# Channel mixers' up panels with tokens stationary, 512 columns each, and results turned and sent by way of the DRAM

## The chip, the cores and the metric

The kernel runs on one core of one Trainium2 chip. Its time is the device time of one execution in microseconds; a lower time is better. The core has a matrix engine (TensorE, PE in the profile, with its weight loads as PEld), a vector engine (VectorE, DVE), a scalar engine (ScalarE, ACT), GpSimd (POOL) and a queue engine that starts most transfers (SyncE, SP). They run side by side and wait for each other on semaphores; each runs its own instructions in the order in which they were built.

## The reference

A trunk of two layers for 256 tokens of width 2048, in float32. The first layer mixes tokens with gated linear attention (GLA), the second with forgetting attention (FoX); both also attend to 256 memory tokens. After each comes a channel mixer, a gated MLP with a causal convolution over three tokens:

```python
def causal_dwconv(u, w, b):
    s_ = u.shape[1]
    up = jnp.pad(u, ((0, 0), (CONV_WIDTH - 1, 0), (0, 0)))
    return w[0] * up[:, 0:s_] + w[1] * up[:, 1:s_ + 1] + w[2] * up[:, 2:s_ + 2] + b

def conv_ffn(h, w_up, conv_w, conv_b, w_down):
    u = causal_dwconv(h @ w_up, conv_w, conv_b)
    a, val = split_cols(u, [FFN_HIDDEN, FFN_HIDDEN])
    return (jax.nn.silu(a) * val) @ w_down

def reference(x, mem, ...):
    mem_n = rmsnorm(mem, norm_mem)
    for i in range(DEPTH):
        if i == N_A_LAYERS:
            fk, fv, fc = fox_shared_kv(x, fox_kv_norm, fox_w_kv, fox_b_f)
        mk, mv = memory_kv(mem_n, mem_w_kv[i])
        h = rmsnorm(x, norm_mix[i])
        ...
        h = rmsnorm(x, norm_ffn[i])
        x = x + conv_ffn(h, ffn_w_up[i], ffn_conv_w[i], ffn_conv_b[i], ffn_w_down[i])
    return rmsnorm(x, norm_final)
```

`h` is 256 x 2048, `w_up` 2048 x 11264 (5632 gate columns, then 5632 value columns), `w_down` 5632 x 2048.

## The kernel before

**Number form.** Every float32 operand of the large products is split in a high part, which TensorE multiplies directly, and the low rest. A product is high x high + high x low + low x high. Activations are kept split as sixteen chunks of 128 inputs (`bufA`, `bufB`, both parts of a chunk side by side, 2 x 256 tokens). Weights are streamed: `split_unit` (L188 to L207) loads a unit of 128 x 1024 numbers into `raw` on SP's queue (L200), copies it to the high part `whi` on ScalarE (L205) and takes the difference `wlo` on VectorE (L206). `raw`, `whi` and `wlo` have four buffers each. `tc.high_priority(offset=AHEAD)` puts the splits ahead in the order that the scheduler builds, so they run before the matmuls that need them.

**Two forms of a product.** `proj_fm` (through `panels_fm`) keeps weights stationary: for a panel of 256 output columns, a unit holds four chunks; the high weights meet both parts of a chunk in one matmul with 512 moving columns (L242), the low weights meet the high part with 256 (L240). The result has columns on partitions and tokens along the row, as high and low sums side by side, which `whole` adds up with one copy on ScalarE (L252) and one addition on VectorE (L254). `proj_tm` keeps 128 tokens stationary: a unit holds two chunks of 512 output columns, which are the moving operand, three matmuls for each chunk and token block (L286). The result has tokens on partitions. `panel_tm` (L311) is the same product in steps of one unit, so that two panels can be interleaved.

**The channel mixer** (`ffn`). The hidden width is done in three parts, `PARTS`, of 16, 16 and 12 blocks of 128. In each part the up panels run first, one for each block, with the block's 128 gate columns and 128 value columns. Their eviction `up_out` adds the halves (`whole`), multiplies with the row of norm factors `nx.row()` (L1038), convolves along the tokens with one ScalarE operation (L1042) and two on VectorE (L1043, L1044), applies SiLU (L1047), multiplies the gate with the value (L1048) and splits the product into the chunk `m[i]` (L352, L353). Then come four down panels of 512 columns, `add_out` with `proj_tm`, which add to the residual `x` (L322). The first three up panels of a mixer are interleaved by `three_fm`, so that the last four chunks of `h` are met late: those come out of the projection just before, through `preparing`.

**Turning.** `preparing` takes each column group `f` (512 columns) of the residual as it is finished, transposes 32 x 32 blocks on VectorE (L1077) and moves the blocks to their partitions with sixteen small DMAs on SP's queue (`move`, L466), then splits them into four chunks (L363, L365). `move_far` (L472, L475), used in the FoX stage, does the same by one DMA to DRAM and four back; SP waits for the first before it starts the four.

**PSUM.** Eight banks: four for `acc`, two for `ps_s`, one each for `ps_o` and `ps_t`.

**The order.** The matmuls stand in program order as far as the scheduler keeps it; `tc.issue_after(i)` puts an instruction behind another one in the built order. After the first mixer comes the FoX stage (keys, values, queries, attention, output projection), then the second mixer and the final norm.

Of the kernel before, what the change touches and what calls it, by code (L numbers as in the profile page):

```python
# [19 lines left out]
P = 128  # L20
# [34 lines left out]
def _panels():  # L55
# [6 lines left out]
    def fm(key, w, c0, kcs=full, second=None):  # L62
        cols = [(c0, 256)] if second is None else [(c0, 128), (second, 128)]
        out.append((key, w, kcs, cols, 4))
# [76 lines left out]
def _trunk(ctx: ExitStack, tc: tile.TileContext, xt, xtok, memt, wp, wgu, gns, gfin, cnv, par, msk, out):  # L141
# [40 lines left out]
    loads, casts, ends = [], [], []  # L182
# [6 lines left out]
    def split_unit(unit, pool=wpool, pieces=1, before=None):  # L189
# [3 lines left out]
        with tc.high_priority(offset=AHEAD):  # L193
# [7 lines left out]
            for i in range(pieces):  # L201
# [4 lines left out]
                V.tensor_tensor(lo[:, s], raw[:, s], hi[:, s].bitcast(F32), ALU.subtract)  # L206
# [86 lines left out]
    def panel_tm(key, src, evac):  # L293
# [24 lines left out]
        return step  # L318

# [149 lines left out]
    def move_far(pool, dst, src, n):  # L469

        far = pool.tile([P, 4 * T], F32, name="far", tag="far", bufs=2)
        nc.sync.dma_start(far[:, : 4 * n], src[:, : 4 * n])  # L472
        blocks = far[:, : 4 * n].rearrange("(q i) (c n) -> c i q n", q=4, c=4)
        for c in range(4):
            nc.sync.dma_start(dst[32 * c : 32 * (c + 1), : 4 * n].rearrange("i (q n) -> i q n", q=4), blocks[c])  # L475
# [538 lines left out]
    def add_out(key, src, then=None, spare=None, last=None, first=0):  # L1014
        for f in range(first, 4):
            def evac(b, a, f=f):
# [4 lines left out]
            proj_tm((*key, f), src, last if f == 3 and last is not None else evac, spare if f == 3 else None)  # L1021

    def ffn(l, nx, h, m, then, spare=None, last=None):
        with tc.tile_pool(name=f"ffn{l}", bufs=1) as fp:
# [6 lines left out]
            for p, (lo, hi) in enumerate(PARTS):  # L1031
                def up_out(j, i):
                    cv = {}

                    def evac(c, a):
                        u = us[turn[0] % 4]
                        turn[0] += 1
                        V.tensor_tensor(u[:, 2:], whole(a), nx.row(), ALU.mult)  # L1038
                        col = (c * 44 + j) * 4
# [6 lines left out]
                        if c == 1:  # L1046
                            S.activation(cv[0], cv[0], AF.Silu)  # L1047
                            V.tensor_tensor(r, cv[0], r, ALU.mult)  # L1048
                            split(m, i, r)
# [182 lines left out]
```

## Time and profile before

| What | Value |
|---|---|
| Median of three runs | 2262.89 us (2262.39 to 2263.41) |
| The profiled execution | 2263.27 us |
| Its span | 2261.4 us |
| TensorE clock granted, mean | 0.999 |
| Instructions | 33526 |
| HBM read | 429.31 MB, 192 GB/s over the span |

The profile was taken on one execution. The time of that execution is 1.9 us above its span, which runs from its first to its last recorded instruction. An engine's busy time counts overlapping instructions once. In lists of groups, a row gives the source line, the engine, the operation, what it writes and reads, the shape and the count, then busy time and the mean duration of one; a matmul's mean duration is longer than the distance between two, because they are pipelined. In the chain of work that ended last, a row gives the start, the length and what ran; its long TensorE pieces divided by their count give the distance of two matmuls. In windows, each engine's busy time is followed by its instruction count, then the granted clock, the share of time that the DMA engines were busy, and GB/s. In a timeline a row gives the start, the length, the engine and the instructions merged into it, and in brackets an idle time before them and what ended it. SPq is SP's queue with the issue of DMAs.

### The profile page before, as it was taken

To read this page: it belongs to the slowest core of one execution; us is meant where nothing else is said; L and a number is where in the kernel's file an instruction comes from. 1 tells how busy PE (TensorE), PEld (TensorE's weight loads), DVE (VectorE), ACT (ScalarE), POOL (GpSimd) and SP (SyncE) were. 2 spreads that over 40 slices of the span, in tenths; PEclk is the share of its full clock that TensorE was granted. 3 is DMA by queue.
4 is the path that set the end of the run, shared out by engine and by line. 5 is a ranking of instruction groups with operands and counts; after the bars stand their busy time and mean duration, and the time that the engine had idled before them with its cause. 6 is when DMAs were issued, how large, how long until landed. Compare 5 with 4: busy or idle time off the path is not lost.

```text
span 2261.4 us, 33526 instructions
## 1 busy us (share of the span) xinstructions
PE 2249.8 (99%) x12253; PEld 1967.1 (87%) x12253; DVE 1617.1 (72%) x2746; ACT 1250.7 (55%) x1986; POOL 3.4 (0%) x19
## 2 busy tenths in 40 slices
PE   9999999999999999999999999999999999999998
PEld 8889998888888888888888998888888888888887
DVE  7779877677765777557777569677776577756775
ACT  6657675555543555445555555456554455534554
POOL 0000000000000000000000000000000000000000
PEclk9999999999999999999999999999999999999999
DMA  9655554665555555555565567766656555655554
GB/s 341 198 184 166 177 168 171 214 201 190 191 196 189 190 193 188 195 188 192 189 217 202 183 192 240 229 204 218 194 189 198 188 189 191 192 194 187 191 193 147
DMA packets 142125, 444.38 MB, mean 197 GB/s; under 512 B 18428, under 2 KB 34952, under 8 KB 141832
## 3 DMA queue, kind: packets, MB, share of 16 engines
q1 hardware_dynamic: 140808, 441.05, 58.8%
q8 instruction: 96, 1.57, 0.3%
q10 hardware_dynamic: 1152, 1.19, 0.2%
q14 instruction: 69, 0.57, 0.1%
HBM read 429.31 MB, written 5.52 MB: 192 GB/s over the span
## 4 chain that ended last, share of the span: by engine, by line
PE 96%; ACT 1%; DVE 1%; DMA 1%; issue 0%; SPq 0%; DVEq 0%; ACTq 0%
PE acc L242 37%; PE acc L286 34%; PE acc L240 20%; PE acc L311 2%; PE ps_s L242 1%; PE ps_s L240 1%; DMA raw<-wp 0%; ACT whi L205 0%; DVE wlo L206 0%; PE ps_s L758 0%; PE ps_o L495 0%; PE ps_s L495 0%; PE ps_o L931 0%; PE ps_s L976 0%; ACT L822 0%
## 5 line engine op out<-in xcount | busy, mean ns | idle before, releaser
L206 DVE TENSOR_TENSOR wlo<-raw,whi 128x1024 fp32r<-128x1024 f32 (+4 forms) x809 | 968.7, 1201 | 518.5 <-ACT whi L205 429.9
L205 ACT ACTIVATE whi<-raw 128x1024 fp32r<-128x1024 f32 (+4 forms) x809 | 839.6, 1039 | 600.5 <-PE acc L286 311.2
L242 PE MATMUL acc<-B,whi 128*128 128x512 f32 x2048 | 482.6, 390 | 0.0
L242 PEld LDWEIGHTS acc<-B,whi 128*128 128x128 f32 x2048 | 378.9, 188 | 75.2
L286 PE MATMUL acc<-whi,mix 128*128 128x512 f32 x1216 | 302.5, 389 | 0.0
L242 PE MATMUL acc<-mix,whi 128*128 128x512 f32 x1224 | 298.3, 391 | 0.0
L286 PEld LDWEIGHTS acc<-whi,mix 128*128 128x128 f32 x1216 | 228.3, 188 | 47.4
L242 PEld LDWEIGHTS acc<-mix,whi 128*128 128x128 f32 x1224 | 226.0, 188 | 44.4
L240 PEld LDWEIGHTS acc<-B,wlo 128*128 128x128 f32 x2048 | 255.7, 191 | 5.3
L240 PE MATMUL acc<-B,wlo 128*128 128x256 f32 x2048 | 259.4, 283 | 0.0
L286 PE MATMUL acc<-whi,B 128*128 128x512 f32 (+3 forms) x896 | 200.5, 360 | 0.0
L286 PEld LDWEIGHTS acc<-whi,B 128*128 128x128 f32 x896 | 162.7, 188 | 15.9 <-ACT whi L205 0.3
L286 PE MATMUL acc<-wlo,mix 128*128 128x512 f32 x608 | 164.5, 389 | 0.0
L240 PEld LDWEIGHTS acc<-mix,wlo 128*128 128x128 f32 x1224 | 154.9, 191 | 6.0 <-ACT mix L363 1.6
L240 PE MATMUL acc<-mix,wlo 128*128 128x256 f32 x1224 | 157.9, 284 | 1.2 <-ACT mix L363 1.2
L286 PEld LDWEIGHTS acc<-wlo,mix 128*128 128x128 f32 x608 | 114.1, 188 | 23.7
L242 PE MATMUL acc<-A,whi 128*128 128x512 f32 x536 | 131.3, 390 | 0.0
L252 ACT ACTIVATE part<-acc 128x256 f32<-128x256 f32 x238 | 89.4, 378 | 58.8 <-PE acc L242 58.8
L242 PEld LDWEIGHTS acc<-A,whi 128*128 128x128 f32 x536 | 100.1, 188 | 20.5
L286 PE MATMUL acc<-wlo,B 128*128 128x512 f32 (+3 forms) x448 | 111.6, 360 | 0.0
L1042 ACT ACTIVATE cv<-u,cw 128x256 f32<-128x256 f32 x176 | 104.2, 595 | 4.2 <-DVE u L1038 4.1
L352 ACT ACTIVATE mix<-cv 128x256 fp32r<-128x256 f32 x60 | 25.0, 416 | 143.6 <-DVE cv L1048 143.6
(250 smaller groups left out, 1809.4 us busy)
## 6 DMA issues: line engine op xcount, KB each, us to landing
raw<-wp SPq DMA_DIRECT2D x743, 512.0 KB, 3.8
raw<-wp SPq DMA_DIRECT2D x32, 384.0 KB, 3.1
raw<-wp SPq DMA_DIRECT2D x24, 388.0 KB, 3.5
turn<-blk SPq DMA_DIRECT2D x144, 32.0 KB, 3.0
raw<-wp SPq DMA_DIRECT2D x8, 400.0 KB, 3.0
far<-y SPq DMA_DIRECT2D x6, 384.0 KB, 6.1
z<-far SPq DMA_DIRECT2D x24, 96.0 KB, 2.9
xf<-xt SPq DMA_DIRECT2D x16, 128.0 KB, 5.2
```

The lines of the kernel that those rows point to most:

```text
L205: casts.append(S.activation(hi[:, s], raw[:, s], AF.Copy))
L206: V.tensor_tensor(lo[:, s], raw[:, s], hi[:, s].bitcast(F32), ALU.subtract)
L240: mm = TE.matmul(acc[p][c][:, :T], w[:, s], both[:, 0, :], start=False, stop=end and j == 3)
L242: mm = TE.matmul(acc[p][c], w[:, s], both, start=u == j == 0, stop=end and j == 3)
L252: S.activation(t, a[:, T:], AF.Copy)
L286: mm = TE.matmul(acc[b][:, :n], src[kcs[j] - base][:, part, b * P : (b + 1) * P], w, start=u == 0 and low == part == j == 0, stop=u == end ...
L311: mm = TE.matmul(acc[b][:, :n], src[kc - base][:, part, b * P : (b + 1) * P], ready[low][:, j * n : (j + 1) * n], start=i == low == part = ...
L352: S.activation(hi, src, AF.Copy)
L1042: S.activation(r, u[:, 2:], AF.Identity, bias=w[3], scale=w[2])
```

## The change

An up panel now has 512 columns: two blocks' gate columns and the same blocks' value columns. It keeps tokens stationary, in `panel_tm`. Its result, tokens on partitions, is transposed in 32 x 32 blocks by VectorE straight from PSUM, high-priority, into one of two buffers `ys`; `far_away` writes that to DRAM with one DMA and returns a function that fetches it back with four, into one of two buffers `zs`. `close` calls that function later: behind the load of the third unit of the panel after next (`issue_after(loads[-1])`), and the convolution behind that unit's low split (`issue_after(lows[-1])`). `convolve` is the old eviction for two blocks, without `whole`; its multiplication with the norm row reads runs of 32 tokens. `ys` and `zs` take over the space of memory keys and values and of FoX's `fvt`, which are free then.

The first two up panels of a mixer are interleaved by `two_tm` in place of `three_fm`: the first six units of both, then the last two of both, with the second one's sums in `ps_s`. The first two down panels of every part are interleaved in the same way, the last unit of each held back, and the last two up panels' fetches and convolutions are put between their units (`hooks`). So the first two column groups of a part end one right after the other. Before FoX they go by `move_far` in place of sixteen small DMAs each.

```diff
         for p, (lo, hi) in enumerate(PARTS):
-            for j in range(lo, hi):
-                fm(("up", l, j), ("ffn_w_up", l), j * P, second=HID + j * P)
+            for j in range(lo, hi, 2):
+                tm(("up", l, j), ("ffn_w_up", l), j * P, 2 * P, more=[(HID + j * P, 2 * P)])
...
-                V.tensor_tensor(lo[:, s], raw[:, s], hi[:, s].bitcast(F32), ALU.subtract)
+                lows.append(V.tensor_tensor(lo[:, s], raw[:, s], hi[:, s].bitcast(F32), ALU.subtract))
...
-    def panel_tm(key, src, evac):
+    def panel_tm(key, src, evac, second=False):
...
-                acc.extend(pacc.tile([P, 512], F32, name="acc", tag="acc") for _ in range(2))
+                acc.extend(work("s", 2) if second else pacc.tile([P, 512], F32, name="acc", tag="acc")
+                           for _ in range(2))
...
+    def two_tm(steps, count, last, hooks={}):
+
+        for units in (range(count - last), range(count - last, count)):
+            for p, step in enumerate(steps):
+                for u in units:
+                    step(u)
+                    hooks.get((p, u), int)()
...
-    def move_far(pool, dst, src, n):
-
-        far = pool.tile([P, 4 * T], F32, name="far", tag="far", bufs=2)
+    def far_away(pool, src, n):
+
+        far = pool.tile([P, 4 * T], F32, name="far", tag="far", bufs=3)
         nc.sync.dma_start(far[:, : 4 * n], src[:, : 4 * n])
         blocks = far[:, : 4 * n].rearrange("(q i) (c n) -> c i q n", q=4, c=4)
-        for c in range(4):
-            nc.sync.dma_start(dst[32 * c : 32 * (c + 1), : 4 * n].rearrange("i (q n) -> i q n", q=4), blocks[c])
+
+        def back(dst):
+            for c in range(4):
+                nc.sync.dma_start(dst[32 * c : 32 * (c + 1), : 4 * n].rearrange("i (q n) -> i q n", q=4), blocks[c])
+
+        return back
+
+    def move_far(pool, dst, src, n):
+        far_away(pool, src, n)(dst)
...
+        if hooks is not None:
+            first = 2
+            two_tm([panel_tm((*key, f), src, evac_of(f), second=f == 1) for f in range(2)],
+                   len(where[(*key, 0)]), 1, hooks)
+        for f in range(first, 4):
+            proj_tm((*key, f), src, last if f == 3 and last is not None else evac_of(f), spare if f == 3 else None)
...
+            def convolve(j, i, z):
+
+                for s in range(2):
                     cv = {}
-
-                    def evac(c, a):
+                    for c in range(2):
                         u = us[turn[0] % 4]
                         turn[0] += 1
-                        V.tensor_tensor(u[:, 2:], whole(a), nx.row(), ALU.mult)
-                        col = (c * 44 + j) * 4
+                        V.tensor_tensor(by_run(u[:, 2:]), z[:, :, 2 * c + s], by_run(nx.row()), ALU.mult)
+                        col = (c * 44 + j + s) * 4
...
+            def up(j, i, second=False):
+
+                def evac(b, a):
+                    with tc.high_priority(offset=AHEAD):
+                        if b == 0:
+                            count[0] += 1
+                        y = ys[count[0] % 2]
+                        V.transpose(y[:, :, :, b, :], a.rearrange("p (k c i) -> p c k i", c=4, i=32))
+                    if b:
+                        open_.append((j, i, far_away(dp, flat(y), T)))
+
+                return panel_tm(("up", l, j), h, evac, second)
+
+            def close(left):
+
+                while len(open_) > left:
+                    j, i, back = open_.pop(0)
+                    z = zs[count[1] % 2]
+                    count[1] += 1
+                    with tc.issue_after(loads[-1].ins):
+                        back(flat(z))
+                    with tc.issue_after(lows[-1].ins):
+                        convolve(j, i, z)
+
+            for p, (lo, hi) in enumerate(PARTS):
+                js = list(range(lo, hi, 2))
                 if p == 0:
-                    first = 3
-                    three_fm([("up", l, j) for j in range(3)], h, [up_out(j, j) for j in range(3)])
-                for j in range(lo + first, hi):
-                    proj_fm(("up", l, j), h, up_out(j, j - lo))
+                    two_tm([up(j, j - lo, j > lo) for j in js[:2]], 8, 2)
+                for n, j in enumerate(js):
+                    if p == 0 and n < 2:
+                        continue
+                    step = up(j, j - lo)
+                    for u in range(8):
+                        step(u)
+                        if p == 0 and n < 4:
+                            if n == 3 and u in (0, 2):
+                                close(2 - u // 2)
+                        elif u == 2:
+                            close(1)
                 end = p == len(PARTS) - 1
-                add_out(("down", l, p), m, then if end else None, spare if end else None, last if end else None)
+                down = {"then": then, "spare": spare, "last": last} if end else {}
+                add_out(("down", l, p), m, hooks={(0, 2): lambda: close(1), (1, 4 if end else 3): lambda: close(0)}, **down)
...
-                move(z, y)
+                if far is not None and f < 2:
+                    move_far(far, flat(z), flat(y), T)
+                else:
+                    move(z, y)
```

More of the change, by code (lines that the diff above doesn't have):

```diff
@@ L1011, in fox, with add_out, evac_of @@
                     steps[f](u)
-    def add_out(key, src, then=None, spare=None, last=None, first=0):
-        for f in range(first, 4):
-            def evac(b, a, f=f):
+    def add_out(key, src, then=None, spare=None, last=None, first=0, hooks=None):
+        def evac_of(f):
+            def evac(b, a):
                 add_to(f)(b, a)
@@ L1158, in last @@
                 (nc.scalar if f == 1 else nc.sync).dma_start(out[b, :, f * 512 + lo : f * 512 + hi], t)
-        ffn(1, n, bufA, bufB, then, op, last)
+        ys, zs = ([const.tile([P, 4, 4, 2, 32], F32, name="yzu", tag=f"{t}{i}") for i in range(2)] for t in ("mk", "mv"))
+        ffn(1, n, bufA, bufB, ys, zs, then, op, last)
 def _constants():
```

46 lines of the change are left out of this document (27 added, 19 removed).

## The prediction

> **What bounds the kernel now.** I read the first part of the page, then the chain of work that ended last, then the list of who made TensorE wait.
>
> ```profile
> span 2261.4 us, 33526 instructions
> PE 2249.8 (99%) x12253; PEld 1967.1 (87%) x12253; DVE 1617.1 (72%) x2746; ACT 1250.7 (55%) x1986; POOL 3.4 (0%) x19
> PE 96%; ACT 1%; DVE 1%; DMA 1%; issue 0%; SPq 0%; DVEq 0%; ACTq 0%
> ```
>
> ```profile
> PE ps_o L180 <- DVE B L177: 1.4, 1, 1.4
> PE acc L240 <- ACT mix L363: 1.2, 1, 1.2
> PE acc L286 <- ACT whi L205: 0.7, 1, 0.7
> PE ps_s L758 <- ACT later L806: 0.3, 1, 0.3
> ```
>
> 96% of the chain is TensorE, and all its recorded waits add up to 1.4 + 1.2 + 0.7 + 0.3 = 3.6 us. So time can come only from what the stream of matmuls itself takes, and be lost only where a new wait breaks it. The next question is what one matmul costs in each form. The chain in order of time shows long pieces that nothing interrupts:
>
> ```profile
> 513.76 7.28 PE acc L242 x32
> 521.04 3.83 PE acc L240 x32
> ...
> 639.66 87.04 PE acc L286 x384
> ```
>
> The first two are one up panel of 256 columns, weights stationary: 32 matmuls with 512 moving columns at 7.28/32 = 0.2275 us, and 32 with 256 at 3.83/32 = 0.1197. The third is a down part, tokens stationary, all matmuls 512 wide: 87.04/384 = 0.2267. Twice the columns cost less than twice the time: the two up rows give (0.2275 - 0.1197)/256 = 0.42 ns a column, and so 0.1197 - 256 x 0.00042 = 0.012 us that every matmul costs whatever its width.
>
> **What is removed: matmuls.** For 512 up columns and one chunk of 128 inputs, before: four 512-wide and four 256-wide; after: six 512-wide. The streamed columns are 3072 both times; two matmuls fewer carry the fixed cost. Per layer 44 panels of 256 become 22 of 512.
> Before: 2 x 44 x (7.28 + 3.83) = 977.7 us. After: 2 x 22 x 16 x 6 = 4224 matmuls x 0.2267 = 957.4 us (by 87.04/384). **Gain 20.2 us.** It needs the down panels' rate to hold beside the up stage's busier VectorE. These two windows, down and up, speak for that:
>
> ```profile
> 640.00:724.00 84.00, 84.00 (x372) 69.60 (x371) 45.67 (x48) 35.51 (x37) 0.00 (x0) 1.00 0.57 195
> 745.00:900.00 155.00, 155.00 (x894) 137.21 (x893) 119.59 (x197) 90.19 (x140) 0.00 (x0) 1.00 0.57 190
> ```
>
> The clock is 1.00 in both, and VectorE at 77% (119.59/155) leaves the up panels at 3.83 and 7.28 us. The rate could be off by 1 ns: 4224 x 0.001 = 4 us to either side.
>
> *A rule against the change.* The Trainium skill (TensorE: Matmul & The Clock Gate, Back-to-back issue gap) puts the fixed cost of a warm matmul at 2.5 ns, not 12. By it the sum would lose almost all its gain: 2 x 16 x 22 x 2 = 1408 matmuls saved x 2.5 ns = 3.5 us. The two rows disagree with it here.
>
> **What is added on VectorE and ScalarE.** These are the groups:
>
> ```profile
> L206 DVE TENSOR_TENSOR wlo<-raw,whi 128x1024 fp32r<-128x1024 f32 x743 | 905.7, 1222 | 471.3 <-ACT whi L205 385.7 <-issue 52.0 <-PE acc L240 20.8
> L205 ACT ACTIVATE whi<-raw 128x1024 fp32r<-128x1024 f32 x743 | 784.0, 1056 | 552.9 <-PE acc L286 275.5 <-PE acc L242 143.4 <-ACT whi L205 47.0
> L254 DVE TENSOR_TENSOR wholes<-acc,part 128x256 f32<-128x256 f32 x238 | 98.9, 418 | 1.0 <-ACT part L252 0.7
> L252 ACT ACTIVATE part<-acc 128x256 f32<-128x256 f32 x238 | 89.4, 378 | 58.8 <-PE acc L242 58.8
> L1038 DVE TENSOR_TENSOR u<-wholes,row 128x256 f32<-128x256 f32 x176 | 74.0, 423 | 2.7
> L1043 DVE SCALAR_TENSOR_TENSOR cv<-u,cw,cv 128x256 f32<-128x256 f32 x176 | 83.7, 478 | 0.0
> L1077 DVE STREAM_TRANSPOSE blk<-x 128x512 f32<-128x512 f32 x24 | 16.9, 706 | 3.7 <-DMA turn<-blk 3.3
> ```
>
> Per 512 columns VectorE loses four additions in `whole` (4 x 0.418 = 1.7 us) and ScalarE four copies (4 x 0.378 = 1.5); VectorE gets two transposes, 2 x 0.706 = 1.4 us by the SBUF row. No row has a transpose that reads PSUM, or a multiplication that picks runs of 32. Bounds: as in these rows (-0.3 us on balance), or twice as long (1.4 us for the transposes, 4 x 0.423 = 1.7 for the products). At the worst VectorE has some 3 us more than before in 21.8 us of TensorE, and it idles 23% (5 us) of the up stage: hidden. I take the low end, since a transpose streams the same 512 elements from either place.
>
> **What is added on the queues.** A panel now writes 512 KB to DRAM in one DMA and fetches it back in four of 128 KB, 44 times. The FoX stage does this already:
>
> ```profile
> far<-y SPq DMA_DIRECT2D x2, 512.0 KB, 5.2
> far<-y SPq DMA_DIRECT2D x6, 384.0 KB, 6.1
> z<-far SPq DMA_DIRECT2D x8, 128.0 KB, 2.9
> raw<-wp SPq DMA_DIRECT2D x743, 512.0 KB, 3.8
> ...
> 1372.80 0.33 SPq L472 DMA_DIRECT2D far<-y  x1
> ...
> 1377.90 1.74 SPq L475 DMA_DIRECT2D z<-far  x4
> ```
>
> There SP waits in line for the write before it issues the fetches (1372.80 to 1377.90), with weight loads behind it, and none of TensorE's four waits lies there. In the up panels the waits are placed late instead. One unit of weights (two chunks) is 12 x 0.2267 = 2.72 us. Call 0 the end of a panel on TensorE. A load of unit k is free to go when the split four units earlier has given up its buffer, which waits for the matmuls eight units earlier: 1.06 + 1.22 = about 2.5 us (with the semaphores) after unit k-8 ends.
> *The write* stands after the load of the next panel's seventh unit (free at -0.2) and waits for the second transpose, about 1.5. The eighth unit's load, behind it, is free at 2.5: nothing lost. *The fetches* stand behind three more loads, the last free at 2.5 + 3 x 2.72 = 10.7; the write has landed at 1.5 + 0.4 + 5.2 = 7.1. No wait; they hold SP for 1.74 us, to 12.4, and the next load is free at 13.4. The data is back at 12.4 + 2.9 = 15.3. *The convolution* stands on VectorE behind the low half of that third unit of the second panel on, which needs the seventh unit of the next panel done (19.0), so it starts at 21.3. Behind it are the splits that TensorE needs, but it finds its data 6 us early. Steady state: **0**. If the write took more than 10.7 - 1.9 = 8.8 us, SP would hold the loads; a load has 10.9 - 2.5 - 3.8 = 4.6 us to spare before the split is late, and the split (2.3 us) has 8.2 - 2.3 = 5.9 before TensorE is. So 10.5 us of cover lie behind the 8.8.
>
> **The joints** are where it can lose.
> *Start of the second mixer.* Now:
>
> ```profile
> 1522.89 3.79 PE L242 MATMUL acc<-mix,whi 128*128 128x512 f32 x16
> 1530.94 0.50 PE L240 MATMUL acc<-mix,wlo 128*128 128x256 f32 x2 [1.19 <-ACT mix L363]
> ...
> 1525.14 11.99 SPq L466 DMA_DIRECT2D turn<-blk  x19
> 1537.23 1.96 SPq L200 DMA_DIRECT2D raw<-wp  x4
> ...
> 1541.02 1.06 ACT L205 ACTIVATE whi<-raw 128x1024 fp32r<-128x1024 f32 x1 [0.68 <-DMA raw<-wp]
> ```
>
> TensorE starts at 1522.89 and meets chunk 8 too early, at 8.1 us. After, chunk 8 is in the fifth unit, at 4 x 2.72 = 10.9: **-1.2 us**. What is late next: SP is held by 19 small moves, only seven loads stand ahead of them in the built program, and the eighth unit's high half ends at 1542.1; it is needed at 1522.89 + 7 x 2.72 + 0.24 = 1542.2. Zero to spare: 0 to 1 us, I take 0.
> *End of the last part* (both mixers). The last panel's convolution waits for unit 9 (counted from 0) of the down part's 24 (needs unit 5's buffers, 16.3 us; start 18.8). Its products and steps are 16 operations of 0.35 to 0.4 us from start to start, 6 us, among four splits of 1.2: 30.4 us. Its chunk would be due at 10 x 2.72 = 27.2, but the built order pulls up unit 12 and two thirds of 13, so the last of it is due at 33.5. Cost 0; 0 to 3 us each if the splits slip.
> *Start of FoX.* The first two down columns now end together, and go to DRAM by `move_far` one after the other. The first is ready 39 us into the part (matmuls done at 35.8; behind them on VectorE an addition, a transpose and a split): write to 45, fetches, second write 48 to 54, fetches to 56.4. Before, the third column's 16 small moves had begun by then (its matmuls end at 18 x 2.72 = 49.0, its transposes 3 us later). Now they end, with five loads between, at 68.7, 3.4 us after FoX starts (65.3), and land at 6.3; the first split of chunk 8 is done at 7.1, and it is due at 6.7. The fourth column's 16 moves follow:
>
> ```profile
> 1190.03 3.79 PE L242 MATMUL acc<-B,whi 128*128 128x512 f32 x16
> ...
> 1192.89 10.62 SPq L466 DMA_DIRECT2D turn<-blk  x16
> ...
> 1215.56 1.06 ACT L205 ACTIVATE whi<-raw 128x1024 fp32r<-128x1024 f32 x1 [2.37 <-DMA raw<-wp]
> ```
>
> They ran from 2.9 to 13.5 us after the start, and ScalarE then waited 2.37 us for a load. After, they run to about 15.5, so the loads behind come 2 us later, into a place that was already short. 0 to 5 us, I take **+2**.
>
> **Sum**, against the profiled execution's own 2263.27 us (span 2261.4 and 1.9 around it): 2263.3 - 20.2 - 1.2 + 2 = 2243.9. The median shown is 0.4 lower than that execution, so I say 2244.
>
> **Rivals.**
> *Joints dearer.* FoX's start costs 5, each last part 3, the second mixer's start 1: 12 where I took 2: about 2254. For it: margins of 0 to 3 us, several at once. Against: before, TensorE lost 1.2 us at all of these.
> *The rate does not carry over* (no change). The up panels mix evictions, transposes and 77% VectorE beside the matmuls; if a 512-wide matmul takes 977.7/4224 = 0.2315 us there, 4.8 ns above the down row, nothing is won: 2263.3 - 1.2 + 2 = 2264. For it: all of the gain is a cost of some 12 ns a matmul whose origin no row names. Against: the down window has the same form, with its splits and evictions, at 0.2267. The Trainium skill's rule above would end near this, at 2260.6.
> *SP blocks (slower).* One mechanism: the write waits for transposes and the fetches for the write on the queue that carries the weights. It decides from a write of 8.8 + 10.5 = 19 us on, or when four fetches and small moves together pass that cover; each us beyond costs 1 us per panel, and 2 us would be 88: 2263.3 - 21 + 88 = 2330; one us, 2286. Against: the longest landing here is 6.1 us for such writes (384 KB, FoX), and these add 1 MB to 21.8 us, 48 GB/s to 190, with DMA engines at 0.57.
> *It doesn't do what it says*: reload of the stationary tokens for each 512 columns is not hidden. The down part has just that, and runs at 0.2267.
>
> **How the numbers follow.** Forecast 0.73 (2244; own range 2240 to 2249), dearer joints 0.17 (2249 to 2258), no change 0.04, slower 0.06. The low end is 2263.3 - 21.4 less half of the rate's 4 us: 2240. The high end takes in the dearer joints and part of the rate: 2256. A measurement of this kernel tells 0.2%, 4.5 us, from no change. Faster 0.90, within it 0.04, slower 0.06.
>
> **What would show it.** Up pieces of the chain at 0.2267 us a matmul, 21.8 us a panel; 1408 matmuls fewer; TensorE's waits under 6 us in all, the largest at FoX's start; SP's wait for the DRAM write gone from the up panels; VectorE's multiplication not waiting for the fetch. I am wrong if the matmul with a stationary token block takes over 0.231 us there, or if TensorE waits for weight splits in each panel.

## The result and the profile after

| | Before | After |
|---|---|---|
| Median | 2263.15 us (4 runs, 2262.39 to 2264.56) | 2246.23 us (4 runs, 2244.61 to 2251.22) |
| Profiled execution | 2263.27 us | 2251.22 us |
| Its span | 2261.4 us | 2249.3 us |

The ratio is 0.9928, with a 95% interval of 0.9911 to 0.9945: 16.9 us faster. The profiled execution of after is the longest of its four, 5 us above their median; the stage where that comes from is shown below. Lines have moved by a few: after, TensorE's matmuls are L313 (tokens stationary, in steps), L285 (tokens stationary) and L241/L239 (weights stationary); the weight split is L204 (ScalarE) and L205 (VectorE); the transposes out of PSUM are L1094, the products with the norm row L1075, the write to DRAM and the fetch L482 and L487, the small moves L476, the splits of turned chunks L373 and L375.

The page of after, its span, its busy times and the chain by engine:

```profile
span 2249.3 us, 30561 instructions
PE 2232.8 (99%) x10845; PEld 1896.4 (84%) x10845; DVE 1589.9 (71%) x2658; ACT 1204.1 (54%) x1810; POOL 3.4 (0%) x19
...
PE 91%; DMA 3%; DVE 2%; ACT 2%; SPq 1%; issue 1%; DVEq 0%; ACTq 0%
```

12253 - 10845 = 1408 matmuls fewer, and TensorE is as full as before. 9% of the chain that ended last is no longer TensorE's (it was 4%); how long TensorE itself waited, the list of its waits below says. The long pieces of the chain in order of time say what an up matmul costs now:

```profile
506.05 149.60 PE acc L313 x660
...
723.65 193.12 PE acc L313 x852
```

193.12/852 = 149.60/660 = 0.2267 us: the rate of the down panels, to the last digit. The stages are told apart by the first matmul of each, in the timeline of TensorE, one row of before (its other two anchors, 1190.03 and 1522.89, stand in the prediction) and three of after:

```profile
461.39 3.79 PE L242 MATMUL acc<-B,whi 128*128 128x512 f32 x16
```

```profile
462.10 1.98 PE L313 MATMUL acc<-whi,B 128*128 128x512 f32 x8
...
1180.44 3.79 PE L241 MATMUL acc<-B,whi 128*128 128x512 f32 x16
...
1520.90 1.98 PE L313 MATMUL acc<-whi,mix 128*128 128x512 f32 x8
```

| Stage | Before, us | After, us | Difference |
|---|---|---|---|
| up to the first mixer | 461.39 | 462.10 | +0.7 |
| first mixer | 728.64 | 718.34 | -10.3 |
| FoX | 332.86 | 340.46 | +7.6 |
| second mixer to the end | 738.51 | 728.40 | -10.1 |

The 0.7 us before the first mixer lie in a part that the change leaves alone: two waits of 0.9 and 0.5 us, which the repeats below don't have, where before there was one of 0.7. The mixers gave 20.4 us and FoX, which the change does not touch but for what feeds its start, took 7.6 back. The list of who made TensorE wait, after:

```profile
PE ps_s L241 <- ACT whi L204: 1.8, 1, 1.8
PE ps_o L179 <- DVE B L176: 1.4, 1, 1.4
PE acc L239 <- ACT B L373: 1.2, 1, 1.2
PE ps_t L442 <- DVE dg L440: 1.1, 1, 1.1
PE acc L239 <- DVE wlo L205: 0.9, 1, 0.9
PE ps_s L313 <- ACT whi L204: 0.5, 1, 0.5
PE acc L285 <- ACT whi L204: 0.5, 1, 0.5
PE ps_s L778 <- ACT later L826: 0.2, 1, 0.2
```

They come to 7.6 us, where before it was 3.6. Each happens once (the second number), so none is a cost of every panel. Three of them, 1.8 + 1.2 + 1.1 = 4.1 us, are at FoX's start. The timeline of TensorE there:

```profile
1188.49 0.51 PE L239 MATMUL acc<-B,wlo 128*128 128x256 f32 x2 [1.18 <-ACT B L373]
...
1205.58 0.38 PE L442 MATMUL ps_t<-dg,onesr 128*128 128x256 f32 x1 [1.10 <-DVE dg L440]
1207.76 3.78 PE L241 MATMUL ps_s<-B,whi 128*128 128x512 f32 x8 [1.80 <-ACT whi L204]
1211.34 1.91 PE L239 MATMUL acc<-B,wlo 128*128 128x256 f32 x8
1213.05 2.42 PE L241 MATMUL acc<-B,whi 128*128 128x512 f32 x8
1215.30 1.11 PE L239 MATMUL acc<-B,wlo 128*128 128x256 f32 x8
1216.26 2.00 PE L241 MATMUL acc<-B,whi 128*128 128x512 f32 x8
```

Eight 512-wide matmuls take 3.78 us at 1207.76 and 2.00 at 1216.26; eight of 256 take 1.91 and then 1.11. Behind the waits TensorE ran slower for some 7 us: (3.78 - 2.00) + (1.91 - 1.11) + (2.42 - 2.00) = 3.0 us lost. The windows show why, in the column behind POOL's, the granted clock:

```profile
1205.00:1210.00 5.00, 2.62 (x6) 2.01 (x7) 5.00 (x8) 2.80 (x4) 0.31 (x1) 0.71 0.59 205
1210.00:1215.00 5.00, 5.00 (x19) 4.29 (x18) 1.81 (x2) 1.06 (x1) 0.00 (x0) 0.61 0.86 306
```

4.1 us of waits and 3.0 of lowered clock are 7.1 of FoX's 7.6 us. What held the engines? First the other queues of after at this place, ScalarE, VectorE and SP:

```profile
1181.61 1.06 ACT L204 ACTIVATE whi<-raw 128x1024 fp32r<-128x1024 f32 x1 [1.93 <-DMA raw<-wp]
...
1206.65 1.06 ACT L204 ACTIVATE whi<-raw 128x1024 fp32r<-128x1024 f32 x1 [1.12 <-DMA raw<-wp]
```

```profile
1181.24 1.13 DVE L375 SCALAR_TENSOR_TENSOR mix<-fvt,gains,mix 128x128 fp32r<-128x128 f32 x4
...
1183.43 1.27 DVE L332 TENSOR_TENSOR x<-x,acc 128x512 f32<-128x512 f32 x2
1184.63 1.22 DVE L205 TENSOR_TENSOR wlo<-raw,whi 128x1024 fp32r<-128x1024 f32 x1
1185.76 1.30 DVE L1145 STREAM_TRANSPOSE blk<-x 128x512 f32<-128x512 f32 x2
```

```profile
1187.80 11.10 SPq L476 DMA_DIRECT2D turn<-blk  x16
1199.01 30.39 SPq L199 DMA_DIRECT2D raw<-wp  x14
```

then VectorE before, at the same place:

```profile
1189.11 0.69 DVE L322 TENSOR_TENSOR x<-x,acc 128x512 f32<-128x512 f32 x1
...
1192.16 0.70 DVE L1077 STREAM_TRANSPOSE blk<-x 128x512 f32<-128x512 f32 x1
```

Counted from FoX's first matmul: before, the fourth group's additions on VectorE began at -0.9 and the last transpose was done at 2.8, so SP's sixteen moves ran from 2.9 to 13.5. After, VectorE's additions begin at 3.0, the transposes end at 6.6, and the moves run from 7.4 to 18.5. They came 5 us later, and every weight load behind them did too.

What VectorE did ahead of the additions were mainly weight splits and the low halves of the first two groups' chunks (L375). It had worked on them without a pause since 1166.42, when the first of these chunks was there, 14 us before FoX's first matmul; before the change the first group's low halves were done 28 us ahead of it. ScalarE's wait of 1.93 us for a weight load, which ends at 1.2, is not what held the additions: its high half is done at 1182.67, so the low half of that unit is at the earliest the one at 1184.63, behind them.

### The profile page after: what moved, and what is told of

Its sections match the earlier page's. It is cut to its first block, busy times and chain, and to the rows that moved or that the text cites. A ratio compares the mean times of both kernels' runs of the same rounds, so it can differ in the third digit from the quotient of the medians.

```text
span 2249.3 us, 30561 instructions
## 1 busy us (share of the span) xinstructions
PE 2232.8 (99%) x10845; PEld 1896.4 (84%) x10845; DVE 1589.9 (71%) x2658; ACT 1204.1 (54%) x1810; POOL 3.4 (0%) x19
## 4 chain that ended last, share of the span: by engine, by line
PE 91%; DMA 3%; DVE 2%; ACT 2%; SPq 1%; issue 1%; DVEq 0%; ACTq 0%
PE acc L313 47%; PE acc L285 22%; PE acc L241 8%; PE ps_s L313 7%; PE acc L239 4%; DMA raw<-wp 3%; DVE wlo L205 1%; ACT whi L204 1%; SPq L476 1%; PE ps_s L778 0%; PE ps_o L515 0%; PE ps_s L515 0%; PE ps_o L951 0%; PE ps_s L996 0%; ACT L842 0%
## 5 line engine op out<-in xcount | busy, mean ns | idle before, releaser
L205 DVE TENSOR_TENSOR wlo<-raw,whi 128x1024 fp32r<-128x1024 f32 (+4 forms) x809 | 966.7, 1197 | 571.4 <-ACT whi L204 545.3
L204 ACT ACTIVATE whi<-raw 128x1024 fp32r<-128x1024 f32 (+4 forms) x809 | 841.6, 1041 | 798.1 <-PE acc L313 376.7
L313 PE MATMUL acc<-whi,B 128*128 128x512 f32 x1488 | 373.3, 389 | 0.0
L313 PEld LDWEIGHTS acc<-whi,B 128*128 128x128 f32 x1488 | 278.9, 188 | 57.6
L313 PE MATMUL acc<-whi,mix 128*128 128x512 f32 x1312 | 325.1, 389 | 0.0
L313 PEld LDWEIGHTS acc<-whi,mix 128*128 128x128 f32 x1312 | 246.1, 188 | 51.0
L313 PE MATMUL acc<-wlo,B 128*128 128x512 f32 x744 | 203.1, 389 | 0.0
L285 PE MATMUL acc<-whi,mix 128*128 128x512 f32 x736 | 183.6, 389 | 0.0
L313 PE MATMUL acc<-wlo,mix 128*128 128x512 f32 x656 | 176.3, 390 | 0.0
L313 PEld LDWEIGHTS acc<-wlo,B 128*128 128x128 f32 x744 | 139.7, 188 | 29.1
L285 PEld LDWEIGHTS acc<-whi,mix 128*128 128x128 f32 x736 | 138.1, 188 | 28.7
L241 PE MATMUL acc<-B,whi 128*128 128x512 f32 x672 | 162.1, 392 | 0.0
L285 PE MATMUL acc<-whi,B 128*128 128x384 f32 (+3 forms) x736 | 160.0, 354 | 0.0
L313 PEld LDWEIGHTS acc<-wlo,mix 128*128 128x128 f32 x656 | 123.1, 188 | 25.5
L241 PEld LDWEIGHTS acc<-B,whi 128*128 128x128 f32 x672 | 123.7, 189 | 24.0
L285 PEld LDWEIGHTS acc<-whi,B 128*128 128x128 f32 x736 | 132.7, 188 | 9.7 <-ACT whi L204 0.3
L285 PE MATMUL acc<-wlo,mix 128*128 128x512 f32 x368 | 100.0, 389 | 0.0
L313 PE MATMUL acc<-whi,A 128*128 128x512 f32 x368 | 94.6, 389 | 0.0
L239 PE MATMUL acc<-B,wlo 128*128 128x256 f32 x672 | 88.6, 285 | 1.2 <-ACT B L373 1.2
L285 PE MATMUL acc<-wlo,B 128*128 128x384 f32 (+3 forms) x368 | 89.3, 354 | 0.0
L239 PEld LDWEIGHTS acc<-B,wlo 128*128 128x128 f32 x672 | 85.9, 193 | 3.8 <-ACT B L373 1.6
```

Source lines behind the costliest of these rows:

```text
L204: casts.append(S.activation(hi[:, s], raw[:, s], AF.Copy))
L205: lows.append(V.tensor_tensor(lo[:, s], raw[:, s], hi[:, s].bitcast(F32), ALU.subtract))
L239: mm = TE.matmul(acc[p][c][:, :T], w[:, s], both[:, 0, :], start=False, stop=end and j == 3)
L241: mm = TE.matmul(acc[p][c], w[:, s], both, start=u == j == 0, stop=end and j == 3)
L285: mm = TE.matmul(acc[b][:, :n], src[kcs[j] - base][:, part, b * P : (b + 1) * P], w, start=u == 0 and low == part == j == 0, stop=u == end ...
L313: mm = TE.matmul(acc[b][:, :n], src[kc - base][:, part, b * P : (b + 1) * P], ready[low][:, j * n : (j + 1) * n], start=i == low == part = ...
```

## The experiments

The runs were made on three chips, each with runs of the kernel before beside them (medians 2262.67, 2262.97 and 2262.92 us). Which kernels share a chip is said where they are compared.

### The changed kernel again

Edit: none.

> The changed kernel once more, to see which part of the 2244.6 to 2251.2 us is the place and which the execution. Theory (stalls at the start of FoX let the clock drop): the waits there, about 4 us, come again, and whether the clock drops (some 3 us more) varies; median 2244 to 2248. Rival (the clock drop is an accident of that one execution and has nothing to do with the place): the granted clock is 1.00 at the start of FoX and lower somewhere else or nowhere; median 2244 to 2246.

Measured: 2248.10 us (5 runs, 2247.36 to 2249.79), 0.1 above the range of the theory, ratio 0.9936 (0.9924 to 0.9949). FoX's start, from its first matmul to the first one of the values' panel (388 wide), takes 66.97 us before, 74.75 in the profiled execution of after and 71.86 here, with 2.4 us of waits and, once more, eight matmuls in 3.68 us behind them, at a granted clock of 0.66. So the place and the mechanism come again, at some 5 us; the 7.6 were a dear execution.

A third time, on the third chip:

> The changed kernel once more, so that the other two stand beside it on the same chip: 2245 to 2250 us, TensorE's waits at FoX's start 2 to 4 us, and a granted clock under 1 for some us there.

Measured: 2248.66 us (2247.53 to 2251.10), ratio 0.9939 (0.9926 to 0.9951), FoX's start 71.58 us. The waits are there, 1.24, 1.37 and 1.13 us, but not the lowered clock; the row of TensorE's timeline and the window:

```profile
1206.71 2.11 PE L241 MATMUL ps_s<-B,whi 128*128 128x512 f32 x8 [1.13 <-ACT whi L204]
```

```profile
1205.00:1210.00 5.00, 3.68 (x19) 3.10 (x20) 5.00 (x7) 2.72 (x4) 0.31 (x1) 1.00 0.61 156
```

The waits belong to the kernel, then; the lowered clock behind them comes in some executions only, against what was expected.

### What a matmul costs whatever its width

Every up matmul of 512 columns, but the first and the last of a sum, is cut in two of 256:

```diff
-                        mm = TE.matmul(acc[b][:, :n], src[kc - base][:, part, b * P : (b + 1) * P],
-                                       ready[low][:, j * n : (j + 1) * n], start=i == low == part == j == 0,
-                                       stop=i == end and low == 1 and j == len(units[i][1]) - 1)
+                        first = i == low == part == j == 0
+                        final = i == end and low == 1 and j == len(units[i][1]) - 1
+                        pieces = 1 if first or final or key[0] != "up" else 2
+                        for q in range(pieces):
+                            c = slice(q * n // pieces, (q + 1) * n // pieces)
+                            mm = TE.matmul(acc[b][:, c], src[kc - base][:, part, b * P : (b + 1) * P],
+                                           ready[low][:, j * n + c.start : j * n + c.stop], start=first, stop=final)
```

> All but the first and the last matmul of each token block of an up panel are cut in two of 256 columns, on the same sums: 44 x 92 = 4048 matmuls more, nothing else changed. Theory (a matmul has a fixed cost of 12 to 14 ns): 4048 x (2 x 0.1197 - 0.2267 us) = 51 us more than the changed kernel, about 2297. Rival (fixed cost 2.5 ns, the gain came from the shorter work on VectorE and ScalarE): 10 us more, 2256. Rival (weight loads bind when every 256 columns need one): over 0.15 us a matmul, more than 2350.

Measured: 2299.05 us (2297.81 to 2300.92), ratio 1.0162 (1.0147 to 1.0178). The page and a piece of the chain:

```profile
PE 2284.0 (99%) x14893; PEld 2105.1 (92%) x14893; DVE 1593.2 (69%) x2658; ACT 1203.2 (52%) x1810; POOL 3.4 (0%) x19
```

```profile
732.35 203.03 PE acc L318 x1588
```

On the chip of the first repeat, 14893 - 10845 = 4048 matmuls more cost 2299.05 - 2248.10 = 51.0 us, 12.6 ns each, with the same numbers streamed and TensorE hardly waiting (busy 99%, and 203.03/1588 = 0.128 us in an intact piece of eight up panels and 84 uncut matmuls of a down panel). The fixed cost that the forecast took from two rows, 12 ns, is thus shown by itself. The Trainium skill (TensorE: Matmul & The Clock Gate, Back-to-back issue gap) gives 2.5 ns for it, in a formula for the gap of an isolated matmul; in a stream of weight loads and matmuls, it says, both set the spacing. By the 2.5 ns this kernel would have lost 4048 x 2.5 ns = 10 us. The measurement decides: not here, with a weight load for every matmul. What the 12 ns are made of no row tells.

### Fetch and convolution at once

Both are put right behind the panel's own write, without the late places:

```diff
                     if b:
                         open_.append((j, i, far_away(dp, flat(y), T)))
+                        close(0)
...
-                    with tc.issue_after(loads[-1].ins):
-                        back(flat(z))
-                    with tc.issue_after(lows[-1].ins):
-                        convolve(j, i, z)
+                    back(flat(z))
+                    convolve(j, i, z)
```

> Each up panel's fetch and convolution stand right behind its write, instead of two panels later. Theory (over 10 us of cover for the loads, and SP waits about 3 us for the write): the up panels keep 0.2267 us a matmul; SP waits in each panel, TensorE doesn't; what is won or lost is at the joints, since the last convolution of a part no longer lies between the down units by hand: within 5 us of the changed kernel, 2243 to 2253. Rival (the lateness is what makes the change work): VectorE's multiplication waits some 8 us for the fetch, the splits behind it are late, TensorE waits 1 us or more in each of 44 panels; over 2290.

Measured, on the second chip: 2379.13 us (2372.99 to 2384.07), ratio 1.0511 (1.0495 to 1.0527), 131 us above the first repeat of the changed kernel. My theory is wrong and the rival right. Who waited on VectorE, and who on TensorE:

```profile
DVE u L1075 <- DMA yzu<-far: 171.7, 21, 10.3
DVE u L1075 <- DMA fvt<-far: 170.8, 21, 10.7
```

```profile
PE acc L313 <- DVE wlo L205: 83.9, 51, 3.7
```

and behind one panel's end in VectorE's timeline:

```profile
777.97 1.44 DVE L1075 TENSOR_TENSOR u<-fvt,row 128x256 f32<-128x256 f32 x4 [4.98 <-DMA fvt<-far]
779.32 1.22 DVE L205 TENSOR_TENSOR wlo<-raw,whi 128x1024 fp32r<-128x1024 f32 x1
```

with the high half of that last split, in ScalarE's:

```profile
773.39 1.06 ACT L204 ACTIVATE whi<-raw 128x1024 fp32r<-128x1024 f32 x1 [1.66 <-PE acc L313]
```

The split at 779.32 could have run from 774.45; it stood behind the product. VectorE stood 171.7 + 170.8 = 342 us, 8 a panel, before a product whose data was on the way, with the weight splits behind it. All of TensorE's waits together come to 98 us (5 in the repeat), and the mean clock is 0.988 where the repeat has 0.998, another 24 us (0.010 x 2378): 117 of the 131; the other 14 have no row of their own.

But SP waits more there too (161 us for the writes). The next kernel tells the two apart: the fetch at once, the convolution in its late place.

```diff
-                        open_.append((j, i, far_away(dp, flat(y), T)))
+                        back, z = far_away(dp, flat(y), T), None
+                        if len(open_) < 2 and all(o[2] is None for o in open_):
+                            z = zs[count[1] % 2]
+                            count[1] += 1
+                            back(flat(z))
+                            back = None
+                        open_.append((j, i, back, z))
...
-                    j, i, back = open_.pop(0)
-                    z = zs[count[1] % 2]
-                    count[1] += 1
-                    with tc.issue_after(loads[-1].ins):
-                        back(flat(z))
+                    j, i, back, z = open_.pop(0)
+                    if back is not None:
+                        z = zs[count[1] % 2]
+                        count[1] += 1
+                        with tc.issue_after(loads[-1].ins):
+                            back(flat(z))
```

> Only the fetches move: they stand in SP's order one and two weight loads behind their panel's DRAM write instead of four; the convolution keeps its late place on VectorE (its order there is the same). Theory V (the kernel with everything at once lost its time through VectorE's waits of some 8 us a panel for the fetched data, with the weight splits behind them): no loss, 2246 to 2250 us, within 2 us of the changed kernel beside it; SP waits some 3 us a panel for the write (over 100 us in all), VectorE's multiplication for nothing, TensorE's waits under 10 us. Theory S (SP's wait for the write, with the weight loads behind it, is what costs): most of the 131 us stay, over 2300 us, and TensorE waits for splits in most panels.

Measured, beside the second repeat of the changed kernel (2248.66): 2247.93 us (2246.50 to 2249.93), ratio 0.9932 (0.9918 to 0.9945). SP's waits for the DRAM:

```profile
SPq L487 <- DMA far<-yzu: 30.1, 16, 5.3
SPq L487 <- DMA far<-yu: 28.5, 16, 3.9
```

SP does wait for the write now, 58.6 us in 32 places (fewer than expected, as one load already stands between), and no time is lost; on VectorE the products wait 2.6 us in all. SP's order around the write and the fetches is the same in both kernels (write, one load, fetches), so it is the convolution's place that makes the difference. The late place of the convolution is what the change needs; the late place of the fetch is not.

### FoX's start: the small moves

Two kernels on the chip of the first repeat. In one the first two groups before FoX go by sixteen small moves each, as before the change:

```diff
-            n2, then = preparing("kv", bufB, tp, turned3, "mix1", dp)
+            n2, then = preparing("kv", bufB, tp, turned3, "mix1")
```

> The first two column groups before FoX go by sixteen small moves each again, and not by way of the DRAM; the rest of the change stays. Theory (SP's queue is held too long ahead of the third group's moves, by the two waits for the DRAM writes, 14.5 us from 1154.5 to 1169): 32 moves at 0.6 us hold it 19 us plus the loads between, so the third group comes some 5 us later and the start of FoX waits 4 to 8 us longer; 2250 to 2256. Rival (the DRAM way's latency is the fault, small moves can be mixed with the loads): the waits there fall under 1 us; 2240 to 2243.

Measured: 2255.28 us (2251.78 to 2256.57), ratio 0.9964 (0.9952 to 0.9976), 7.2 us above the changed kernel. The fourth group's moves run to 1213.1, and TensorE waits 4.1 and 3.2 us; FoX's start takes 78.9 us.

In the other both writes to DRAM stand ahead of both fetches, so that SP does not stand in line for the first write with the second behind it:

```diff
                 if far is not None and f < 2:
-                    move_far(far, flat(z), flat(y), T)
+                    sent.append((f, z, far_away(far, flat(y), T)))
+                    if f == 0:
+                        return
+                    for _, to, back in sent:
+                        back(flat(to))
                 else:
                     move(z, y)
-                for k in range(4):
-                    split_turned(dst, 4 * f + k, z, name)
+                for g, to, _ in sent if f == 1 and sent else [(f, z, None)]:
+                    for k in range(4):
+                        split_turned(dst, 4 * g + k, to, name)
```

> Before FoX both column groups are written to the DRAM first and only then fetched, so SP waits for the writes once and not twice. Theory (SP held by two waits): SP is free about 5 us earlier, chunk 8 is there when TensorE wants it, the loads behind the last moves come earlier too; the waits at the start of FoX fall from 4.1 us to under 1.5, no clock drop; 2240 to 2244. Rival (the two groups that end together burden VectorE and ScalarE, SP is not it): waits stay within 1 us of 4.1, time within 2 us of the changed kernel.

Measured: 2249.51 us (2249.12 to 2251.91), ratio 0.9942 (0.9930 to 0.9955): no gain, as the rival had it, and FoX's start takes 73.5 us. Chunk 8's wait is gone, but one wait of 4.0 us for a split stands there instead. The waits for the two writes are not what is late. Counted from FoX's first matmul, the third group's moves end at 2.1 (2.4 in the first repeat), and yet VectorE begins the fourth group's additions at 3.5 (2.3) and ends its transposes at 9.3 (6.0), so its moves run from 9.3 to 19.9 (6.5 to 17.6).

Three kernels on the second chip relieve SP at that place in different ways. All four groups by way of the DRAM:

```diff
-                if far is not None and f < 2:
+                if far is not None:
                     move_far(far, flat(z), flat(y), T)
```

> Before FoX all four column groups go by way of the DRAM: five DMAs each, no small moves. Theory (SP's queue is held by the 16 + 16 small moves, 10 and 11 us, and the loads behind them are late; where the loads or the row factors come late, the clock drops on top): SP is held 3 to 5 us for each group, the loads behind come 6 us earlier, waits at the start of FoX under 1.5 us and clock 1.00 there; 2240 to 2244. Rival (not SP's time but the late end of the two groups and the crowd on VectorE): waits and time within 2 us of the changed kernel, 2246 to 2250.

Six of the sixteen moves of every fourth group that goes by small moves issued by ScalarE (`some` picks them):

```diff
+                elif f == 3:
+                    move(z, y, some)
                 else:
                     move(z, y)
```

> Of the sixteen small moves of each fourth column group (before the first mixer, FoX and the second mixer) six start from ScalarE's queue. Theory (SP's time holds the loads): SP is held 7 us instead of 11, the loads behind come 4 us earlier, the wait for the split at the start of FoX (1.0 and 1.8 us) goes, so does the drop of the clock; 2241 to 2245. Rival (ScalarE, which makes the high halves, loses as much by waiting for the transposes at the head of its queue): no change or slower, 2247 to 2252.

And all groups by way of the DRAM at the other two joints as well (the first edit, with a DRAM pool for each):

> All four column groups go by way of the DRAM at all three joints. By the theory of SP's time: as with the four groups before FoX alone, and the 0.5 to 1 us of wait at the start of the second mixer goes as well: 2239 to 2243. Rival (a round trip of 9 to 12 us is longer than sixteen small moves where little stands ahead): the first mixer's start, which waits for nothing now, gets a wait of 1 to 3 us; 2243 to 2248.

| Kernel | Median, us | Ratio, 95% interval | FoX's start, us |
|---|---|---|---|
| all four groups by DRAM | 2244.48 (2244.27 to 2244.85) | 0.9917 (0.9904 to 0.9931) | 67.6 |
| six moves on ScalarE | 2244.35 (2242.88 to 2245.11) | 0.9916 (0.9902 to 0.9929) | 68.1 |
| DRAM at all joints | 2244.06 (2241.48 to 2247.91) | 0.9918 (0.9905 to 0.9932) | 69.8 |

Each is 3.6 to 4.0 us below the first repeat, and FoX's start is 0.6 to 2.8 us above the 66.97 us of before. The second came within the range of its theory; the first ended 0.5 us above it. The third ended in the range of its rival, but not by the rival's wait: the first mixer's start waits for nothing, and at FoX's start TensorE waits 1.4 and 0.9 us. So the other two joints brought no more. As that repeat ran on another chip, one of them was run again beside the changed kernel:

> All four groups before FoX by way of the DRAM, on the same chip as the changed kernel. If SP's small moves hold the loads at FoX's start, it is 3 to 5 us below the changed kernel beside it, with the clock at 1.00 through FoX's start; if the two jobs before differed by their chips, it is within 1 us of it.

Measured: 2244.39 us (2242.38 to 2245.08), ratio 0.9916 (0.9903 to 0.9930), against 2248.66 (2247.53 to 2251.10) beside it: 4.3 us. FoX's start takes 66.95 us against 71.58, 4.6 less, and TensorE waits for nothing there. SP in the first run of this kernel:

```profile
1176.06 16.20 SPq L199 DMA_DIRECT2D raw<-wp  x6
1192.56 0.33 SPq L482 DMA_DIRECT2D far<-blk  x1
1193.66 1.54 SPq L199 DMA_DIRECT2D raw<-wp  x2
1197.33 1.75 SPq L487 DMA_DIRECT2D turn<-far  x4
```

and the clock there:

```profile
1205.00:1210.00 5.00, 5.00 (x27) 4.28 (x27) 5.00 (x15) 4.37 (x10) 0.29 (x1) 1.00 0.58 207
```

One write of 0.33 us and fetches of 1.75 stand where 11.10 us of moves stood, six weight loads go ahead of the write and two between it and the fetches, and the clock stays at 1.00. That SP's time in small moves at FoX's start is what cost those 4 to 5 us is shown by taking it away (by the DRAM twice, by ScalarE once) and by adding to it in one kernel. VectorE is no earlier for it: in the run beside the changed kernel its transposes of the fourth group end 11.6 us after FoX's first matmul. So, as far as these runs show, their lateness costs time only with 11 us of moves behind them on the queue that carries the weights. These kernels beat both the kernel before and the changed one; that putting the two remedies together brings more was not tried.

## Why the prediction was right

**The forecast** was 2244, the result 2246.23: right side, right mechanism, 2.2 us off. That it came so close is partly luck: the repeats of the same kernel, 2248.10 and 2248.66, lie 4.1 and 4.7 us above it, still inside the range. Most of the miss is in one term, FoX's start.

*Matmuls removed, 20.2 us.* Right. The up pieces run at 0.2267 us a matmul, the doubtful carrying-over of the rate held, and the first mixer, for which the sum had no other term, gave 10.3 us, where half of the forecast is 10.1. The rival by which nothing carries over is refuted by the pieces of the chain, and the fixed cost it doubted was measured by itself, 12.6 ns.

*VectorE and ScalarE, hidden.* Right, at the low end of both bounds. The groups of after, and the window of the up stage:

```profile
L1075 DVE TENSOR_TENSOR u<-fvt,row 128x256 f32<-128x256 f32 x88 | 31.5, 418 | 1.5 <-DMA fvt<-far 1.4
L1094 DVE STREAM_TRANSPOSE yu<-acc 128x512 f32<-128x512 f32 x42 | 29.7, 708 | 1.9 <-PE acc L313 1.9
```

```profile
745.00:900.00 155.00, 155.00 (x685) 128.36 (x684) 113.00 (x173) 82.69 (x110) 0.00 (x0) 1.00 0.78 241
```

The transpose out of PSUM takes 708 ns where the SBUF row had 706, the product that picks runs of 32 takes 418 ns; VectorE fell from 119.59 to 113.00 us of 155 and TensorE is full. One product waited for its fetch, 1.4 us.

*The queues, 0.* Right in the sum, with two sizes off, both the safe way or covered. The issues of DMAs:

```profile
far<-yu SPq DMA_DIRECT2D x22, 512.0 KB, 2.8
...
yzu<-far SPq DMA_DIRECT2D x88, 128.0 KB, 6.1
```

The write lands in 2.8 us instead of 5.2, the fetch in 6.1 instead of 2.9. In one panel SP's timeline and VectorE's give the room that was left:

```profile
755.42 1.85 SPq L487 DMA_DIRECT2D fvt<-far  x4
```

```profile
765.81 1.43 DVE L1075 TENSOR_TENSOR u<-fvt,row 128x256 f32<-128x256 f32 x4
```

Issued by 757.27, back by 763.0 to 763.3 (these four took 5.7 to 6.0 us), used at 765.81: some 2.5 us early, not 6. SP's wait for the write to land is gone from the up panels, as forecast. The blocking rival (SP) did not come, and the kernel with the fetch at once shows that waits of SP of up to 5.3 us are covered; whether 10.5 are, as reckoned, was not tried. What the prediction did not price was the other half: the same lateness on VectorE, whose product waits in line ahead of the splits. That is the half that would have cost 131 us.

*Second mixer's start, -1.2.* Nearly: the wait at chunk 8 is gone, and the eighth unit, "zero to spare", was 0.53 us late (1.0 and 0.7 in the repeats), within its 0 to 1. From its first matmul to the kernel's last, 2253.49 before and 2240.54 after, the mixer became 11.0 us shorter. Behind the last matmul the kernel then took 8.8 us where it had taken 7.9: 0.9 us that the sum did not have, and whose cause was not looked for.

*End of the last part, 0.* Right: no wait of TensorE lies there.

*Start of FoX, +2 (0 to 5).* The term that was mis-sized: +4.6 to +4.9 in the two repeats, +7.8 in the profiled execution. The late split of chunk 8 was seen (1.18 us of wait there), and so was the end of the third group's moves (3.4 us after FoX's start in the forecast, 4.0 in the trace). The step that failed is "After, they run to about 15.5": they ran to 18.5 (17.6 and 17.4 in the repeats). I moved the fourth group's moves by the third group's alone and left VectorE out: the moves wait for its transposes, and these, behind the low halves of the first two groups' chunks, were done at 6.6 and not at 2.8. That what stood ahead made VectorE late is read from its rows; no run took that work away. The kernel with both writes first, where the third group's moves end earlier and the fourth group's transposes later, speaks against late moves or loads as the cause. On top came the lowered clock, which I had no term for. With 4.7 in place of 2, the sum would have been 2246.6.

*Waits under 6 us in all, the largest at FoX's start*: 7.6 us in the profiled execution, 5.0 and 5.8 in the repeats. The three at FoX's start make the largest share, where it was said to be.

## What to carry to other kernels

Where TensorE is full, fewer and wider matmuls are worth their number times the fixed cost of one, read from two widths in the trace, and the evictions that this forces elsewhere cost nothing here, where each engine's queue had room for them. When a result makes a round trip, put its first user late on the engine that uses it, not only the fetch late on the queue: an early fetch was free here, an early user cost 131 us. And when a stage speeds up, look at the joint behind it, engine by engine: the moves at FoX's start were reckoned from the queue that starts them, and the engine that feeds them was left out. That was most of the error here.

## What the runs showed of the hardware

- A matmul with its own weight load costs 12 to 13 ns beside its columns, in this stream: 51.0 us for 4048 more.
- After 1.10 and 1.80 us of waits with one short matmul between them the clock was granted at 0.71 and 0.61 in the two 5 us windows from 1205 on, and 3.0 us were lost; in the first repeat 1.11 and 1.00 us at the same place brought 0.66, in the second 1.37 and 1.13 us left it at 1.00. The Trainium skill (TensorE: Matmul & The Clock Gate, What's actually happening) has the clock set by a free-running window of some 3.4 us. The rows agree so far as that the drop depends on more than the length of the waits; that the window's phase decides it was not tested.
- A write of 512 KB to DRAM landed in 2.8 us here while fetches of 128 KB to 32 partitions took 5.7 to 6.1; with the fetches issued right behind the write, they took 4.2 to 4.3, and the write 2.9 to 3.1. What sets these times stays open.
- VectorE passed nothing ahead of a product that waited for its data (4.98 us at 777.97, with the split behind it ready from 774.45). The Trainium skill (Perfetto Trace Analysis, Tensor Engine Instruction) says that VectorE's queue is strictly first in, first out; this trace agrees.
